# A hybrid decoder block on one core: weight halves and activation tiles moved by 64 bytes against each other

## The chip, the cores and the metric

The kernel runs on one NeuronCore of a Trainium2 chip, as one launch. The metric is the device time of an execution in microseconds; 1 us is 1000 ns. Every number on the kernel before comes from three timed executions, or from one further execution that the hardware profiler recorded.

## The reference, cut to what matters

For 256 tokens of width 2048 the block computes, in float32 (cut to its matrix products):

```python
h = rms_norm(x, attn_norm_g)
q, k, v, u, gate_attn, gate_ssm = split(h @ w_in + b_in)
attn = sliding_window_attention(q, k, v, sinks)
y_val, y_gate = split(gelu(s5_ssm(u, ...)) @ w_glu + b_glu)
ssm = y_val * sigmoid(y_gate)
merged = sigmoid(gate_attn) * (attn @ w_branch_attn) + sigmoid(gate_ssm) * (ssm @ w_branch_ssm)
x = x + merged @ w_out
val, gate = split(rms_norm(x, ffn_norm_g) @ w_up)
x = x + (val * gelu(causal_depthwise_conv(gate))) @ w_down
return rms_norm(x, final_norm_g)
```

Nearly all of the arithmetic is in seven products of 256 tokens with large weight matrices: `w_in`, `w_branch_attn`, `w_glu`, `w_branch_ssm`, `w_out`, `w_up`, `w_down`.

## The kernel before

**Units.** All weights are cut into 416 units of 128 partitions x 1024 columns, in the order that `_units` (line 58) lists: `q0`, `u`, `kv`, `q1`, `ga`, `gs` (parts of `w_in`), `A` (`w_branch_attn`), `glu`, `S` (`w_branch_ssm`), `o` (`w_out`), `up0` to `up21` (`w_up`), `dn0` to `dn3` (`w_down`). A unit is eight blocks of 128 x 128. The loop at line 1009 goes through the units; TensorE is fed by it without a break, and the other work (the state-space scan, attention, norms) is put in between by generators (`fill`, line 802) as soon as a hand-kept clock of each engine says that its inputs are there.

**Split numbers.** Each float32 weight is split into two parts that TensorE multiplies at its fast float32 rate: `load` (line 220) brings a unit into one of four buffers `raw`, each as soon as the buffer's last unit is split; `prep` (line 231) lets ScalarE round it into `whi` (the upper half) and VectorE compute `wlo = raw - whi` (the lower half). There are five buffers of each (`LOOK = 5`), used in turn. The activations are split in the same way into an upper and a lower tile. A product is hi x hi + hi x lo + lo x hi.

**Two shapes of the inner loop.** TensorE holds a block of weights (128 x 128) and streams columns of activations past it; while one block is in use, the next block is loaded (profile engine PEld). Where the accumulator has 256 columns (all stages up to `up0`, and `dn3`), three matmuls of 256 columns are made per block, lines 1064 to 1066: `whi` past the upper activations, `whi` past the lower, `wlo` past the upper. Where it has 512 columns (`up1` to `up21`, `dn0` to `dn2`; `double`, line 1051), the activation tile holds upper and lower side by side, and two matmuls are made:

```python
PE.matmul(acc[:, c], hi[:, kk, c], both, ...)              # 512 columns, upper half of the weights
PE.matmul(acc[:, c, 0:T], lo[:, kk, c], mh[:, k], ...)     # 256 columns, lower half
```

So in the wide stages a load of a lower half lies under each matmul of 512 columns, and a load of an upper half under each of 256. In the narrow stages a load lies under every matmul of 256 columns. This text calls a matmul, from its start to the start of the next, a step, and the two steps of a block in the wide stages a pair.

**Where the tiles lie.** Each tile has an address, the byte at which it starts in every partition. Tiles are laid down one behind the other by pools, so a tile that grows moves all behind it. Blocks of weights lie 512 bytes apart within a unit, and the parts of activation tiles 1024 or 2048 bytes apart, so a tile's start over the last multiple of 128 bytes (its offset, below) is that of each of its operands too. In the kernel before `whi` and `wlo` have offset 0 in all five buffers; `xg` and `x2g` (lines 183 and 968: inputs of `q` to `gs`, and of `up`) have 64; `ath`/`atl` (input of `A`), `su` (`glu`), `mh`/`ml` (`o`) and `H` (`dn`) have 0; `sy` (`S`) has 96.

Of the kernel before, what the change touches and what calls it, by code (L numbers as in the profile page):

```python
# [8 lines left out]
F32 = mybir.dt.float32  # L9
F32R = mybir.dt.float32r  # L10
# [5 lines left out]
P = 128  # L16
T = 256
NK = 16
D_MODEL = 2048
D_FF = 5632  # L20
NFF = D_FF // P
EPS = 1e-6
NJ = 16
LOOK = 5
# [33 lines left out]
def _units():  # L58
# [7 lines left out]
    out = pair(block("q0", NK, 4), block("u", NK, 4)) + block("kv", NK, 2) + block("q1", NK, 4)  # L66
    for n, K in (("ga", NK), ("gs", NK), ("A", 8)):
        for c in range(3 if n == "A" else 4):
            out += block(f"{n}{c}", K, 4)
# [68 lines left out]
def hybrid_block_kernel(  # L138
# [17 lines left out]
    base = ctx.enter_context(tc.tile_pool(name="base", bufs=1))  # L156
    strm = ctx.enter_context(tc.tile_pool(name="strm", bufs=1))
# [22 lines left out]
    ident = base.tile([P, P], F32, tag="ident", name="ident")  # L180
    rs = base.tile([P, T], F32, tag="rs", name="rs1")
    hb = base.tile([P, 40], F32, tag="hb", name="hb")
    A = base.tile([P, NK, 2, T], F32R, tag="A", name="xg")
    Ah, Al = A[:, :, 0], A[:, :, 1]
    mid_cm, mid = open_pool("mid")
    X = mid.tile([P, NK, T], F32, tag="tS", name="x_in")
# [18 lines left out]
    units = _units()  # L205
# [25 lines left out]
    def prep(i, parts=1):  # L231
        if i >= NU:
            return
        raw = raws.pop(i)
        clk_a.ns = max(clk_a.ns, clk_pe.ns if i >= LOOK else 0.0, arrive.pop(i))
        hi = strm.tile([P, 1024], F32R, tag="whi", name=f"whi{i}", bufs=LOOK)
        lo = strm.tile([P, 1024], F32R, tag="wlo", name=f"wlo{i}", bufs=LOOK)
        n = 1024 // parts
        for j in range(parts):
            sl = slice(j * n, (j + 1) * n)  # L240
            S.copy(hi[:, sl], raw[:, sl])
            clk_v.ns = max(clk_v.ns, clk_a.ns + 130.0)
            V.tensor_tensor(lo[:, sl], raw[:, sl], hi[:, sl].bitcast(F32), op=ALU.subtract)
        prepped[i] = (hi, lo, clk_v.ns)
        if i >= 4:
            load(i + 4)
# [30 lines left out]
        V.tensor_tensor(sq[:, 0:2], sq[:, 0:2], sq[:, 2:4], op=ALU.add)  # L277
        V.tensor_tensor(sq[:, 0], sq[:, 0], sq[:, 1], op=ALU.add)

# [1 line left out]
    V.memset(ones, 1.0)  # L281
    V.memset(eps, EPS)
    S.activation(hb[:, 0:1], eps, AF.Sqrt)
# [10 lines left out]
    warm = bank("at", P)  # L294
    for i in range(WARM):
        PE.matmul(warm, ones, ones, start=True, stop=True)
# [1 line left out]
    st = {}  # L298
    bq8 = base.tile([P, 8], F32, tag="bq8", name="bq8")

    def ev_proj(name, acc, dst, scale, biases, func, fscale):
# [6 lines left out]
        def rest():  # L308
            for i in range(m):
                yield "A", None  # L310
                S.activation(dst[:, i], dst[:, i], func, bias=biases[i], scale=fscale)
# [17 lines left out]
        ks = range(4 * b, 4 * b + 4)  # L329
        ev_proj(f"{n}{b}", acc, dst[:, 4 * b : 4 * b + 4], None, [hb[:, off + i : off + i + 1] for i in ks], AF.Tanh, 0.5)  # L330

# [1 line left out]
    def g_norm1():  # L333
        sq = mid.tile([P, 2, 4, T], F32, tag="tA", name="sq1")
        v = p1.tile([P, 2], F32, tag="sv1", name="sv1")
# [2 lines left out]
        dg = p1.tile([P, 2, P], F32, tag="ul", name="dg")  # L338
        yield "A", None
        S.activation(sq[:, 0], X[:, 0:4], AF.Square)  # L340
        for b in range(1, 4):
            yield "A", None
            S.activation(sq[:, 1], X[:, 4 * b : 4 * b + 4], AF.Square)
# [23 lines left out]
        S.copy(rs, ps[1].rearrange("p h t -> p (h t)"))  # L367
        st["rs"] = True

# [1 line left out]
    def g_ssm():  # L371
        sp = p1.tile([P, 22, NJ], F32, tag="sp", name="sp")
        ki = p1.tile([P, NJ], I32, tag="ki", name="ki")
# [59 lines left out]
        dt, mag, th, n, r, sn, cn, sh, abr, abi, zr, zi, t1, t2, t3, t4, den, ar = [t(i) for i in range(18)]  # L433
# [19 lines left out]
        tt(zr, t1, den, ALU.mult)  # L453
        yield "D", None

        E = base.tile([P, 2, NJ, P], F32, tag="X", name="E")
        V.memset(E[:, 0, :, 0:1], 1.0)
        V.memset(E[:, 1, :, 0:1], 0.0)
        V.tensor_copy(E[:, 0, :, 1:2], cn.unsqueeze(2))
        V.tensor_copy(E[:, 1, :, 1:2], sn.unsqueeze(2))  # L460
        L = 1
        while L < P:
# [3 lines left out]
            for j0 in range(0, NJ, jn):  # L466
                js = slice(j0, j0 + jn)
                a = p1.tile([P, 2, jn, cnt], F32, tag="T1", name=f"ea{L}_{j0}", bufs=2)
                b = p1.tile([P, 2, jn, cnt], F32, tag="T2", name=f"eb{L}_{j0}", bufs=2)
                lr = E[:, 0:1, js, L : L + 1].to_broadcast([P, 2, jn, cnt])  # L470
                li = E[:, 1:2, js, L : L + 1].to_broadcast([P, 2, jn, cnt])
                src = E[:, :, js, 1 : cnt + 1]
# [153 lines left out]
        y_ev(3)  # L626
        st["y3"] = True

# [1 line left out]
    def g_attn():  # L630
        yield "D", wait_for("kv", "q0")
        qT = st["qT"]
# [88 lines left out]
    def g_norm2():  # L721
        sq, ps = st["sq"], {}
        yield "D", None
        fold(sq)

        def total():
            ps[0] = bank("at", 2)
            for h in range(2):
                PE.matmul(ps[0][:, h : h + 1], sq[:, 0, h * P : (h + 1) * P], ones[:, 0:1], start=True, stop=True)

        def spread():
            ps[1] = bank("at", 2, P)
            for h in range(2):
                PE.matmul(ps[1][:, h], ones, dg[:, h], start=True, stop=True)

        yield "D", later(total)
        n2 = mid.tile([P, 3, 2], F32, tag="ath", name="n2")
        dg = mid.tile([P, 2, P], F32, tag="atl", name="dg2")
        rstd(ps[0], n2[:, 0], n2[:, 1], n2[:, 2])
        for h in range(2):  # L740
            V.tensor_scalar(dg[:, h], ident, n2[:, 2, h : h + 1], None, op0=ALU.mult)
        yield "A", later(spread)
        st["rs2"] = base.tile([P, T], F32, tag="rs", name="rs2")
        S.copy(st["rs2"], ps[1].rearrange("p h t -> p (h t)"))
        close_pool(st["p2cm"])
        close_pool(mid_cm)
        st["ffncm"], fp = open_pool("ffn")
        st["ffn"] = fp
        st["H"] = fp.tile([P, NFF, 2, T], F32R, tag="H", name="H")
        st["gb"] = fp.tile([P, 2, T + 2], F32, tag="gb", name="gb")  # L750
        V.memset(st["gb"][:, :, 0:2], 0.0)

# [172 lines left out]
    def evac(name, acc):  # L925
        if name == "u":
            ev_u(acc)
        elif name == "kv":
            ev_kv(acc)
            spawn(g_attn(), dve=5000.0, act=5000.0, first=True)  # L930
        elif name[0] == "q":
            ev_q(int(name[1]), acc)
        elif name[:2] == "ga":
            if st["tA"] is None:
                st["tA"] = mid.tile([P, NK, T], F32, tag="tA", name="tA")
            ev_gate("ga", st["tA"], int(name[2]), 0, acc)
        elif name[:2] == "gs":
            if st["tS"] is None:
                st["tS"] = mid.tile([P, NK, T], F32, tag="tS", name="tS")
            ev_gate("gs", st["tS"], int(name[2]), 16, acc)  # L940
        elif name[0] == "A":
            ev_A(4 * int(name[1]) + (2 if name[-1] == "y" else 0), 2 if len(name) == 3 else 4, acc)
        elif name[0] == "S":
            ev_S(int(name[1]), acc)
        elif name[:3] == "glu":
            if name == "glu0":
                assert not gens and not aux
                close_pool(p1_cm)
                st["p2cm"], st["p2"] = open_pool("p2")
                p2 = st["p2"]  # L950
                st["mh"] = p2.tile([P, NK, T], F32R, tag="mh", name="mh")
                st["ml"] = p2.tile([P, NK, T], F32R, tag="ml", name="ml")
                st["sy"] = base.tile([P, 2, 4, T], F32R, tag="X", name="sy")
            ev_glu(int(name[3]), acc)
        elif name[0] == "o":
            ev_o(int(name[1]), acc)
        elif name[:2] == "up":
            ev_up(int(name[2:]), acc)
        elif name[:2] == "dn":
            ev_dn(int(name[2]), acc)  # L960

    def begin(name):
        if name == "glu0":
            finish("su1")
        elif name == "o0":
            st["X"] = base.tile([P, NK, T], F32, tag="X", name="xres")
            nc.gpsimd.dma_start(st["X"], xT)
            A2 = base.tile([P, NK, 2, T], F32R, tag="A", name="x2g")
            st["A"], st["Ah"], st["Al"] = A2, A2[:, :, 0], A2[:, :, 1]
            A2 = mid.tile([P, 2, 4, T], F32, tag="tA", name="sqA")  # L970
            st["sq"], st["sq2"] = A2[:, 0], A2[:, 1]
        elif name == "dn0":
            A3 = base.tile([P, 2, NK, T], F32, tag="A", name="xo_sq")
            st["xo"] = A3[:, 0]
            st["sq"], st["sq2"] = A3[:, 1, 0:4], A3[:, 1, 4:8]

# [32 lines left out]
    for i, (name, K, m, k0, kw) in enumerate(units):  # L1009
        if k0 == 0:  # L1010
# [11 lines left out]
            if name[:2] == "dn" or name[:2] == "up" and name != "up0":  # L1022
                if name == "up1":
                    close_pool(ax_cm)
                    wide_cm, pool = open_pool("wide_b", space=PSUM, side="right")
                    wide = [pool]
                elif name == "up2":
                    close_pool(acc_cm)
                    wide_cm2, pool = open_pool("wide_a", space=PSUM, side="left")
# [3 lines left out]
            elif name == "kv":  # L1033
                accs[name] = bank("pq", m, T)
            elif name[:2] == "A3":
                accs[name] = bank("at" if name == "A3x" else "pq", m, T)
# [6 lines left out]
        hi, lo, ready = prepped.pop(i)  # L1043
        clk_pe.ns = max(clk_pe.ns, ready)
        hi = hi.rearrange("p (k m c) -> p k m c", k=kw, m=m)
        lo = lo.rearrange("p (k m c) -> p k m c", k=kw, m=m)
# [11 lines left out]
        for kk in range(0 if double else kw):  # L1058
            k = k0 + kk
            for c in range(m):  # L1060
                o = acc[:, c, 0:T]
                first = k == 0 and (c % 2 == 0 or name == "dn3")
                last = k == K - 1
# [27 lines left out]
        if k0 + kw == K and name == "dn2":  # L1091
            spawn(g_pre(), 2)

# [1 line left out]
    Hh, Hl = st["H"][:, :, 0], st["H"][:, :, 1]  # L1095
    Xr, xo, sq = st["X"], st["xo"], st["sq"]
    n3 = st["ffn"].tile([P, 3, 2], F32, tag="cy", name="n3")
# [12 lines left out]
    for n in range(4):  # L1110
        o = (aux, acc)[n % 2][:, n // 2 * 2, 0:T]
# [23 lines left out]
    for c0, c1 in zip(cuts, cuts[1:]):  # L1135
        o = xo[:, c0:c1]
# [102 lines left out]
```

## Time and profile before

| what | value |
|---|---|
| three timed executions | 1251.51, 1252.0, 1253.03 us (median 1252.0) |
| profiled execution, first to last instruction | 1249.7 us |
| stage `o`, 768 steps of 256 columns | 92.15 us |
| stages `up`, from 502.60 us on | 482.71 us, 2757 matmuls |
| stages `dn`, up to the tail | 241.27 us, 1512 matmuls |
| VectorE, ScalarE busy | 856.9 us, 620.0 us |

The profiled execution's own time is its span of 1249.7 us; the timed executions hold some 2.3 us more around it. PE is TensorE's matmuls, PEld its weight loads, DVE VectorE, ACT ScalarE. The recorded duration of a matmul reaches past the start of the next one, since matmuls are pipelined; what a step costs is read from the chain of work that ended last (start, length, number of matmuls).

### The profile page before, as it was taken

What the parts mean: (1) busy time and instruction counts of PE and PEld (TensorE: products, weight loads), DVE (VectorE), ACT (ScalarE), POOL (GpSimd) and SP (SyncE); (2) the same over time, 40 slices, a digit from 0 to 9 for tenths busy, and PEclk for the clock granted to TensorE, in tenths of its full rate; (3) what the DMA queues carried; (4) which work ended last, traced back from release to release, by engine and by line L of the source; (5) the groups of instructions that cost most, each with busy time, mean ns of one, the idle gap of its engine ahead of it and who ended that gap; (6) DMA issues with size and microseconds to landing.
All of it is one profiled execution on the core that took longest, in us unless ns stands there. A gap on an engine that the chain in (4) does not pass through costs nothing.

```text
span 1249.7 us, 20901 instructions
## 1 busy us (share of the span) xinstructions
PE 1235.7 (99%) x8476; PEld 1125.1 (90%) x8476; DVE 856.9 (69%) x1220; ACT 620.0 (50%) x865; POOL 10.4 (1%) x24
## 2 busy tenths in 40 slices
PE   9999999999999999999999999999999999999996
PEld 8999899989999999988888888888888888888996
DVE  7988998989878556567677666676666755454543
ACT  7676555554444445445445454454455534343531
POOL 0000000000000000000000000000000000000000
PEclk9999999999999999999999999999999999999998
DMA  8565444444446654654655646546456475646451
GB/s 315 205 203 185 162 152 162 140 164 169 153 169 227 207 180 163 205 183 152 214 174 179 216 145 216 189 159 222 159 187 214 140 235 165 208 165 208 165 184 68
DMA packets 64896, 228.29 MB, mean 183 GB/s; under 512 B 7648, under 2 KB 9056, under 8 KB 64672
## 3 DMA queue, kind: packets, MB, share of 16 engines
q1 hardware_dynamic: 63648, 223.55, 52.9%
q0 software_dynamic: 1152, 3.41, 0.9%
q8 instruction: 66, 1.08, 0.4%
q14 instruction: 30, 0.25, 0.1%
HBM read 224.31 MB, written 2.10 MB: 181 GB/s over the span
## 4 chain that ended last, share of the span: by engine, by line
PE 98%; DVE 1%; DMA 0%; ACT 0%; SPq 0%; issue 0%; DVEq 0%
PE acc_up L132 40%; PE acc_dn L132 20%; PE acc_o L132 7%; PE acc_gs L132 7%; PE acc_ga L132 7%; PE acc_q L132 3%; PE acc_A L132 3%; PE pq L132 2%; PE at L132 2%; PE acc_u L132 2%; PE acc_S L132 2%; PE yp L132 1%; PE acc_glu L132 1%; PE aux L132 1%; DMA raw<-in_wst_dram 0%; DVE xo_sq L132 0%
## 5 line engine op out<-in xcount | busy, mean ns | idle before, releaser
L132 DVE TENSOR_TENSOR wlo<-raw,whi 128x1024 fp32r<-128x1024 f32 (+2 forms) x421 | 501.4, 1209 | 277.0 <-ACT whi L132 274.0
L132 ACT CAST whi<-raw 128x1024 fp32r<-128x1024 f32 (+2 forms) x421 | 429.5, 1038 | 420.4 <-PE acc_dn L132 111.3
L132 PE MATMUL acc_up<-x2g,whi 128*128 128x512 f32 (+1 forms) x1472 | 497.2, 387 | 0.0
L132 PE MATMUL acc_up<-x2g,wlo 128*128 128x256 f32 x1408 | 395.4, 281 | 0.0
L132 PEld LDWEIGHTS acc_up<-x2g,whi 128*128 128x128 f32 x1472 | 272.1, 188 | 62.4
L132 PEld LDWEIGHTS acc_up<-x2g,wlo 128*128 128x128 f32 x1408 | 264.3, 188 | 0.0
L132 PE MATMUL acc_dn<-H,whi 128*128 128x512 f32 (+1 forms) x856 | 245.9, 355 | 0.0
L132 PE MATMUL acc_dn<-H,wlo 128*128 128x256 f32 x692 | 194.7, 281 | 0.0
L132 PEld LDWEIGHTS acc_dn<-H,whi 128*128 128x128 f32 x856 | 150.4, 189 | 24.8
L132 PEld LDWEIGHTS acc_dn<-H,wlo 128*128 128x128 f32 x692 | 131.3, 190 | 0.0
L132 PE MATMUL acc_gs<-xg,whi 128*128 128x256 f32 x512 | 91.4, 282 | 0.0
L132 PE MATMUL acc_ga<-xg,whi 128*128 128x256 f32 x512 | 91.2, 282 | 0.0
L132 PEld LDWEIGHTS acc_gs<-xg,whi 128*128 128x128 f32 x512 | 77.8, 189 | 2.6 <-issue 1.7
L132 PEld LDWEIGHTS acc_ga<-xg,whi 128*128 128x128 f32 x512 | 77.6, 188 | 2.8 <-issue 2.0
L132 PE MATMUL acc_o<-mh,whi 128*128 128x256 f32 x256 | 72.5, 283 | 0.0
L132 PE MATMUL acc_o<-ml,whi 128*128 128x256 f32 x256 | 72.5, 283 | 0.0
L132 PE MATMUL acc_o<-mh,wlo 128*128 128x256 f32 x256 | 72.5, 283 | 0.0
L132 PE MATMUL acc_gs<-xg,wlo 128*128 128x256 f32 x256 | 71.3, 278 | 0.0
L132 PE MATMUL acc_ga<-xg,wlo 128*128 128x256 f32 x256 | 71.2, 278 | 0.0
L132 PEld LDWEIGHTS acc_o<-ml,whi 128*128 128x128 f32 x256 | 49.2, 192 | 0.0
L132 PEld LDWEIGHTS acc_o<-mh,whi 128*128 128x128 f32 x256 | 49.2, 192 | 0.0
L132 PEld LDWEIGHTS acc_o<-mh,wlo 128*128 128x128 f32 x256 | 49.2, 192 | 0.0
(212 smaller groups left out, 1371.7 us busy)
## 6 DMA issues: line engine op xcount, KB each, us to landing
raw<-in_wst_dram SPq DMA_DIRECT2D x415, 512.0 KB, 4.2
xres<-in_xT_dram POOLq DMA_DIRECT2D x1, 2048.0 KB, 9.9
x_in<-in_xT_dram SPq DMA_DIRECT2D x7, 256.0 KB, 5.9
out_dram<-xo_sq SPq DMA_DIRECT2D x7, 256.0 KB, 2.4
br<-in_ssmb_dram POOLq DMA_DIRECT2D x3, 256.0 KB, 4.2
raw<-in_wst_dram SPq DMA_DIRECT2D x2, 256.0 KB, 3.4
cT<-in_ssmc_dram SPq DMA_DIRECT2D x1, 512.0 KB, 6.3
us<-ul POOLq DMA_DIRECT2D x16, 32.0 KB, 3.1
```

Of the source, the lines that this page charges most:

```text
L132: return fn(*a, **k)
```

## The change

The change alters addresses alone. On each of the five engines the instructions and their order are the same before and after; no matmul, load, copy or transfer is added, removed or moved in order.

- A helper `shifted` makes a tile 16 elements (64 bytes) larger and uses it from element `off` on. It is used for `xg`, `E`, `xres`, `xo_sq` (off 0), `x2g` and `H` (off 16) and `sy` (off 8).
- A `wlo` buffer becomes 1040 elements long, so that the five begin at offsets 0, 64, 0, 64, 0, and `prep` uses 1024 of them from element 0 or 16 on: in the stages `up` and `dn` so that the lower half lies at offset 64, in all others at 0.
- Since tiles grow, those behind them move. `ath`, `atl`, `su`, `mh`, `ml` come to lie at offset 64, and the small tiles of the state-space branch and of attention all move by 64, moving and stationary operands alike. `raw`, which began at a multiple of 256 bytes, begins 128 bytes over one.

Offsets in bytes over a multiple of 128, before and after:

| stage | activations | `whi` | `wlo` |
|---|---|---|---|
| `q`, `u`, `kv`, `ga`, `gs` | 64, 64 | 0, 0 | 0, 0 |
| `A`, `glu`, `o` | 0, 64 | 0, 0 | 0, 0 |
| `S` | 96, 64 | 0, 0 | 0, 0 |
| `up` | 64, 0 | 0, 0 | 0, 64 |
| `dn` | 0, 0 | 0, 0 | 0, 64 |

The core of the diff:

```diff
-    A = base.tile([P, NK, 2, T], F32R, tag="A", name="xg")
+
+    def shifted(pool, tag, name, dims, dtype, off=0, room=16):
+        n = math.prod(dims)
+        t = pool.tile([P, n + room], dtype, tag=tag, name=name)[:, off : off + n]
+        names = "abcd"[: len(dims)]
+        return t.rearrange(f"p ({' '.join(names)}) -> p {' '.join(names)}", **dict(zip(names, dims)))
+
+    A = shifted(base, "A", "xg", (NK, 2, T), F32R)
...
-        lo = strm.tile([P, 1024], F32R, tag="wlo", name=f"wlo{i}", bufs=LOOK)
+        o = 16 if (i % LOOK % 2 == 0) == (units[i][0][:2] in ("up", "dn")) else 0
+        lo = strm.tile([P, 1040], F32R, tag="wlo", name=f"wlo{i}", bufs=LOOK)[:, o : o + 1024]
...
-        E = base.tile([P, 2, NJ, P], F32, tag="X", name="E")
+        E = shifted(base, "X", "E", (2, NJ, P), F32)
...
-        st["H"] = fp.tile([P, NFF, 2, T], F32R, tag="H", name="H")
+        st["H"] = shifted(fp, "H", "H", (NFF, 2, T), F32R, 16)
...
-                st["sy"] = base.tile([P, 2, 4, T], F32R, tag="X", name="sy")
+                st["sy"] = shifted(base, "X", "sy", (2, 4, T), F32R, 8)
...
-            st["X"] = base.tile([P, NK, T], F32, tag="X", name="xres")
+            st["X"] = shifted(base, "X", "xres", (NK, T), F32)
...
-            A2 = base.tile([P, NK, 2, T], F32R, tag="A", name="x2g")
+            A2 = shifted(base, "A", "x2g", (NK, 2, T), F32R, 16)
...
-            A3 = base.tile([P, 2, NK, T], F32, tag="A", name="xo_sq")
+            A3 = shifted(base, "A", "xo_sq", (2, NK, T), F32)
```

## The prediction

> **What bounds the kernel now.** I read the page first: who is busy, the clock, and the chain of work that ended last. DVE is VectorE and ACT ScalarE.
>
> ```profile
> PE 1235.7 (99%) x8476; PEld 1125.1 (90%) x8476; DVE 856.9 (69%) x1220; ACT 620.0 (50%) x865; POOL 10.4 (1%) x24
> PEclk9999999999999999999999999999999999999998
> PE 98%; DVE 1%; DMA 0%; ACT 0%; SPq 0%; issue 0%; DVEq 0%
> ```
>
> TensorE's matmuls make up 98% of the chain, at the full granted clock. Nobody feeds it late, so the time is the number of steps by the length of a step, and the change leaves the number as it is. The question is whether a step's length depends on where its operands lie. The chain in order of time answers that for 256 columns (start, length, number of matmuls):
>
> ```profile
> 12.96 2.72 PE acc_q L132 x24
> 52.15 10.88 PE pq L132 x96
> 101.55 13.82 PE acc_ga L132 x120
> 167.34 5.30 PE acc_ga L132 x45
> 363.15 8.64 PE acc_glu L132 x72
> 371.79 8.41 PE acc_S L132 x71
> 395.41 92.15 PE acc_o L132 x768
> ```
>
> The matmul has one shape throughout, and yet the step differs. Activations at offset 64, weights at 0: 2.72/24 = 113.3 ns in `q`, 10.88/96 = 113.3 in `kv` (pq), 115.2 and 117.8 in the two pieces of `ga`. Activations and weights both at 0: 8.64/72 = 120.0 in `glu`, 92.15/768 = 120.0 in `o`. In between, at 96 (`S`): 118.5. So 113.3 is the free step, equal offsets cost 6.7 ns, and unequal ones cost nothing in one mode and 4.5 ns in another (117.8). As 256 columns take 113.3 ns, 6.7 ns is the time of 15 of them, and 16 columns are 64 bytes: it looks as if one stream waits until the other has passed its piece of 64 bytes.
>
> Now the wide stages, 58% of the span, with the recorded duration of one matmul by shape:
>
> ```profile
> 502.60 482.71 PE acc_up L132 x2757
> 985.31 241.27 PE acc_dn L132 x1512
> L132 PE MATMUL acc_up<-x2g,whi 128*128 128x512 f32 x1344 | 474.9, 397 | 0.0
> L132 PE MATMUL acc_up<-x2g,wlo 128*128 128x256 f32 x1408 | 395.4, 281 | 0.0
> L132 PE MATMUL acc_dn<-H,whi 128*128 128x512 f32 x528 | 186.6, 399 | 0.0
> L132 PE MATMUL acc_dn<-H,wlo 128*128 128x256 f32 x692 | 194.7, 281 | 0.0
> ```
>
> Of the 2757 matmuls of `up`, 2688 are 1344 pairs, and 69 belong to `up0` (7.8 us at 113.3): (482.71 - 7.8)/1344 = 353.3 ns a pair. Of `dn`, 456 belong to `dn3` (54.7 us at 120.0): (241.27 - 54.7)/528 = 353.3. Unequal offsets in `up`, equal ones in `dn`, and the same pair. Free, 768 columns would take three times 113.3, 340.0. So each pair loses 13.3 ns, twice the 6.7 of above, whichever the offsets, as long as both weight halves have the same one.
>
> **Why, by the loads.** The first matmul of 512 columns, alone in its window, with its neighbours; the free 256-column group of `kv`; and the loads of `up`, whose last column is the idle time before them:
>
> ```profile
> L132 PE MATMUL acc_up<-x2g,whi 128*128 128x512 f32 x1 | 0.4, 388 | 0.0
> L132 PE MATMUL pq<-xg,whi 128*128 128x256 f32 x64 | 10.9, 276 | 0.0
> L132 PEld LDWEIGHTS acc_up<-x2g,whi 128*128 128x128 f32 x1472 | 272.1, 188 | 62.4
> L132 PEld LDWEIGHTS acc_up<-x2g,wlo 128*128 128x128 f32 x1408 | 264.3, 188 | 0.0
> ```
>
> A load takes 188 ns, longer than a narrow step: there each load follows on the one before, 75 ns into its step (188 - 113). I call that chained. The load of a lower half, under 512 columns, is chained too (idle 0.0). The load of an upper half, under 256 columns, is not: before it the loader stood idle, 62.4 us/1344 = 46 ns each time, so it begins with its step. I call that fresh. The first matmul of 512 columns came straight out of the narrow rhythm of `up0`, chained and with unequal offsets, and lasted 388, which is 276 and the 112 of another 256 columns: free. All later ones last 397, and their 256-column partners 281 where 276 is free: +9 and +5, together the 13.3 within rounding. So unequal offsets suit a chained load, and a fresh one collides with them; I conclude that a fresh load wants equal offsets, and that its delay puts the next chained one out of step.
>
> **The change part by part.** *Wide stages.* `x2g` and `H` at 0, `whi` at 0, `wlo` at 64: the fresh load of `whi` gets equal offsets and the chained load of `wlo` unequal ones. If both collisions go, the pair is 340.0: (1344 + 528) x 13.3 = 24.9 us saved. No row of before shows mixed halves. The ends are 340.0, the free pair, and above it 360, since the narrow steps at equal offsets lose 6.7 for each of 256 columns (3 x 120.0). I take 340.0: the first 512-column row shows that half of it exists. Against it: in `dn` the fresh loads have equal offsets already and their matmuls still average 281. There the chained loads collide (399 against 388), which may disturb the fresh ones.
>
> *Narrow stages that go from equal to unequal.* `A` 384 steps, `glu` 96, `o` 768, so 1248. They come to the offsets of `q` and `ga`, between 113.3 and 117.8; I take 115.2, the longest `ga` piece quoted: 1248 x 4.8 = 6.0 us (2.7 to 8.3). `S`, 192 steps from 118.5: 0.6 us (0.1 to 1.0).
>
> *Narrow steps with mixed halves.* `up0` (192 steps) and `dn3` (528 with its tail) have chained loads alone; of three, two bring `whi` (equal, 120.0) and one `wlo` (unequal, 113.3): 117.8 on average. `dn3`: 528 x 2.2 = 1.2 us saved; `up0`, from 115.2: 192 x 2.6 = 0.5 us lost.
>
> *All else* stays: `q` to `gs` keep their offsets, and the small matmuls of attention and the scan have both operands moved by 64. At a pair of 340 a unit takes 2.72 us where it took 2.83. The other engines in the wide stages (busy us of PE, PEld, DVE, ACT, POOL, then clock, DMA share, GB/s):
>
> ```profile
> 430.00:700.00 270.00, 270.00 (x1754) 245.04 (x1753) 175.15 (x207) 132.64 (x163) 0.00 (x0) 1.00 0.55 185
> raw<-in_wst_dram SPq DMA_DIRECT2D x415, 512.0 KB, 4.2
> xres<-in_xT_dram POOLq DMA_DIRECT2D x1, 2048.0 KB, 9.9
> 3.07 5.71 DMA raw<-in_wst_dram
> ```
>
> VectorE is busy 65% and the DMA engines 55%; 4% more is no bound. The `raw` buffers now begin 128 bytes over a multiple of 256. `xres` already begins off such a multiple (224 over), and its 2048 KB land in 9.9 us, not slower per byte than `raw` (512 KB in 4.2), so I cost that at nothing. Only the first load, 5.71 us on the path, has no cover. The Trainium skill, "DMA: Bandwidth & Descriptors", section "How a descriptor splits into AXI transactions", speaks against the change here: a descriptor that doesn't start on 256 bytes needs one transaction more, 17 in place of 16 for 4096 bytes. By that page the uncovered load would be an estimated 0.4 us longer and the sum as much less; the `xres` row doesn't show it.
>
> **Sum.** 24.9 + 6.0 + 0.6 + 1.2 - 0.5 = 32.2 us. The profiled span of 1249.7 would become 1217.5. The timed median is 1252.0, 2.3 more, which stays: 1219.8, rounded to 1220. With the narrow bounds (3.4 to 10.0) this case spans 1217 to 1224.
>
> **Rivals.**
> 1. *Half of it.* One of the two collisions goes, the pair is 346.7: 12.5 + 7.3 = 19.8, 1232. For it: the two are separate in the rows (+9, +5). Against: the later one seems caused by the earlier.
> 2. *The pair doesn't move.* For it: 353.3 at two quite different offsets; the +9 on 512 columns could come with the shape once it runs, and the first one be an exception. Then the narrow stages alone gain: 1252.0 - 7.3 = 1244.7 (1242 to 1249).
> 3. *Slower: the load of `whi` collides at equal offsets whether fresh or chained*, as every narrow step of `o` does, and sets the next load off its place. The pair becomes the 360 of three steps of `o`: 1872 x 6.7 = 12.5 lost, 7.3 won, 1257. It decides from a pair of 353.3 + 7300/1872 = 357.2 on. For it: `up` gives up the unequal offsets that are the better ones in every narrow row. Against: `dn`, all equal, is at 353.3 and not at 360.
> 4. *Slower: the period is 256 bytes, not 128.* In before `xg` lies 192 over a multiple of 256 and the weights 0; after, `whi` lies at 128, and `q` to `gs`, 2208 steps, would fall to 120.0: 2208 x 4.8 = 10.6 lost, the gains in `A`, `glu` and `o` not made, and if the pairs stay too, 1263. Against: 6.7 ns fits 64 bytes, not 128.
> 5. *The change does nothing*, since loads and moving columns don't meet in memory: 1252. The rows speak against it: 113.3 and 120.0 for one shape. The Trainium skill, "TensorE: Matmul & The Clock Gate", Part 2, says so of the load of the next block: it "doesn't steal SBUF read bandwidth from the running matmul". By that rule the sum is 0; the trace disagrees with it, if it is the load that the columns meet.
>
> **How the numbers follow.** Forecast 46%, rival 1 14%, rival 2 20%, rival 3 11%, rival 4 4%, rival 5 5%. Forecast and rivals 1 and 2 hold 80%, so the range runs from 1215 (the forecast's lower end less the 1.5 us by which the runs differ) to 1249. A measurement of this kernel can tell about 0.2%, 2.5 us, from no change. Faster: 0.46 + 0.14 + 0.20 = 0.80. Same: 0.05. Slower: 0.11 + 0.04 = 0.15.
>
> **What would show it.** Right: the 512-column group of `up` at a mean of 388 and its partners at 276, `up` and `dn` alike; the idle time before the loads of `whi` down to some 39 ns each (227 - 188); the chain piece of `o` at 87 to 90 us. Rival 1: one of the two groups alone shorter. Rival 2: 397 and 281 stay. Rival 3: 403 and 283 or more. Rival 4: `kv` above 113.3. The forecast is wrong if the pair is above 347.

## The result, and the profile after

| | before | after |
|---|---|---|
| timed executions | 1251.51 to 1253.03 us (four) | 1244.58, 1244.64, 1245.79 us |
| median | 1252.1 us | 1244.6 us |
| profiled execution, first to last instruction | 1249.7 us | 1244.0 us |
| last matmul's start, from the span's start | 1240.4 us | 1234.9 us |

The ratio is 0.9946, with an interval of 0.993 to 0.9962: 0.5% faster, where the prediction said 2.6%. A fourth execution of after took 1333.55 us at a granted clock of 0.85 and is left out here; the profiled one shows a clock of 0.95, but its steps have the length that experiment 2 has at 1.00 (117.8 ns in `o`).

The page of after: busy time of the engines, the shares of the chain that ended last, the shapes in the wide stages, and the transfers of `raw`.

```profile
PE 1230.2 (99%) x8476; PEld 1127.4 (91%) x8476; DVE 857.7 (69%) x1220; ACT 620.0 (50%) x865; POOL 10.4 (1%) x24
PE 96%; DVE 2%; DMA 1%; ACT 1%; issue 0%; SPq 0%; DVEq 0%; ACTq 0%
L132 PE MATMUL acc_up<-x2g,whi 128*128 128x512 f32 x1344 | 468.2, 392 | 0.0
L132 PE MATMUL acc_up<-x2g,wlo 128*128 128x256 f32 x1408 | 395.5, 281 | 0.2 <-DVE wlo L132 0.2
L132 PEld LDWEIGHTS acc_up<-x2g,whi 128*128 128x128 f32 x1472 | 271.9, 188 | 56.5
raw<-in_wst_dram SPq DMA_DIRECT2D x415, 512.0 KB, 4.3
```

The same 8476 matmuls; TensorE is still the bound, and the time is still their number by the length of a step. The loader stands idle for 56.5 us ahead of the loads of upper halves where it was 62.4, and the matmul of 512 columns went from 397 to 392 ns, but its partner of 256 columns still averages 281. One of the two groups alone is shorter: that is the sign which the prediction gave for its rival 1. The chain in order of time (start, length, number of matmuls):

```profile
13.21 2.80 PE acc_q L132 x24
53.72 11.31 PE pq L132 x96
104.18 14.34 PE acc_ga L132 x120
400.98 90.46 PE acc_o L132 x768
506.82 219.78 PE acc_up L132 x1284
983.60 237.90 PE acc_dn L132 x1512
```

Three things are to be seen. `kv` (pq) and the long piece of `ga`, whose offsets over 128 did not change, went from 113.3 and 115.2 ns a step to 11.31/96 = 117.8 and 14.34/120 = 119.5 (117.8 over the whole of `ga`). `o` came down from 120.0 to 90.46/768 = 117.8, not to 115.2. And the pair of the wide stages is shorter, by less than foretold: in `dn`, with 456 steps of `dn3` at 118.5, (237.90 - 54.0)/528 = 348.2 ns.

Summed over every step of a stage, from one matmul's start to the next one's (us; in brackets the mean step or pair in ns, waits left out):

| stage | before | after | difference | forecast |
|---|---|---|---|---|
| `up1` to `up21`, `dn0` to `dn2`: 1872 pairs | 661.4 (353.3) | 652.5 (348.3) | -8.9 | -24.9 |
| `q`, `u`, `kv`, `ga`, `gs` | 263.3 (115.0) | 269.1 (117.7) | +5.8 | 0 |
| `A`, `glu`, `o` | 150.6 (119.9) | 148.1 (117.9) | -2.6 | -6.0 |
| `S` | 23.6 (118.4) | 23.3 (116.3) | -0.3 | -0.6 |
| `dn3` with its tail | 63.6 (120.0) | 62.8 (118.5) | -0.8 | -1.2 |
| `up0` | 22.2 (114.4) | 22.8 (117.8) | +0.6 | +0.5 |
| everything else | | | +0.6 | 0 |
| sum | | | -5.6 | -32.2 |

So two things have to be explained: why the pair is 348.3 and not 340, and why the stages that were to stay as they were lost 5.8 us.

**In two units of five the change does the opposite of what it says.** Here are the starts of three units of `up1`, each of 8 pairs (start, recorded length, line, operation, tiles); the matmuls between them are left out:

```profile
517.57 0.39 PE L132 MATMUL acc_up<-x2g,whi 128*128 128x512 f32 x1
...
523.17 0.39 PE L132 MATMUL acc_up<-x2g,whi 128*128 128x512 f32 x1
...
531.50 0.39 PE L132 MATMUL acc_up<-x2g,whi 128*128 128x512 f32 x1
```

From the first to the second lie two units, 16 pairs of 350.0 ns; from the second to the third three units, 24 pairs of 347.1. Over all of `up`, by the unit's number modulo 5, the pairs are 346.7, 349.4, 351.0, 347.2 and 347.1 ns. The addresses in the built kernel tell why: the pool hands out the five `wlo` buffers in the order first, fifth, fourth, second, third, while the formula in `prep` takes them to come first to fifth. For units 1 and 2 modulo 5 the lower half therefore lies at 0 in the wide stages and at 64 in the narrow ones. The table of offsets ahead of the prediction holds for the other three units only.

### The profile page after: what moved, and what is told of

It is laid out like the page before. It is cut to its first block, busy times and chain, and to the rows that moved or that the text cites. A ratio compares the mean times of both kernels' runs of the same rounds, so it can differ in the third digit from the quotient of the medians.

```text
span 1244.0 us, 20901 instructions
## 1 busy us (share of the span) xinstructions
PE 1230.2 (99%) x8476; PEld 1127.4 (91%) x8476; DVE 857.7 (69%) x1220; ACT 620.0 (50%) x865; POOL 10.4 (1%) x24
## 4 chain that ended last, share of the span: by engine, by line
PE 96%; DVE 2%; DMA 1%; ACT 1%; issue 0%; SPq 0%; DVEq 0%; ACTq 0%
PE acc_up L132 37%; PE acc_dn L132 19%; PE acc_ga L132 7%; PE acc_gs L132 7%; PE acc_o L132 7%; PE acc_q L132 3%; PE acc_A L132 3%; PE pq L132 2%; PE at L132 2%; PE acc_u L132 2%; PE acc_S L132 2%; PE yp L132 1%; DMA raw<-in_wst_dram 1%; PE acc_glu L132 1%; DVE wlo L132 1%; PE aux L132 1%
## 5 line engine op out<-in xcount | busy, mean ns | idle before, releaser
L132 PE MATMUL acc_up<-x2g,whi 128*128 128x512 f32 (+1 forms) x1472 | 491.1, 383 | 0.0
L132 PEld LDWEIGHTS acc_up<-x2g,whi 128*128 128x128 f32 x1472 | 271.9, 188 | 56.5
L132 PE MATMUL acc_dn<-H,whi 128*128 128x512 f32 (+1 forms) x856 | 242.5, 350 | 0.0
L132 PEld LDWEIGHTS acc_dn<-H,whi 128*128 128x128 f32 x856 | 149.4, 188 | 22.2
L132 ACT ACTIVATE cy<-cy 128x512 f32<-128x512 f32 x22 | 13.9, 632 | 69.9 <-DVE cy L132 69.9
L132 PEld LDWEIGHTS acc_gs<-xg,wlo 128*128 128x128 f32 x256 | 48.1, 188 | 0.0
```

Of the source, the lines that this page charges most:

```text
L132: return fn(*a, **k)
```

## The experiments

From here on *distance* is the start of the activations less the start of `whi`, and *lower distance* the start of `wlo` less that of `whi`, both modulo 256 bytes. Before: `q` to `gs` and `up` have distance 192, `A`, `glu`, `o` and `dn` 0, `S` 224, lower distance 0 everywhere. After: 64 in `q` to `gs`, `A`, `glu`, `o`, 192 in `S`, and 128 in `up` and `dn`; the lower distance in the wide stages is 64 or 192 in three units of five, and 0 in two. Theories: (A) the prediction's, offsets modulo 128; (B) the period is 256 bytes; and, of the pair, whether the wrong units alone keep it from 340.

**1. The formula mended.**

```diff
-        o = 16 if (i % LOOK % 2 == 0) == (units[i][0][:2] in ("up", "dn")) else 0
+        o = 16 if (i % LOOK in (0, 1, 4)) == (units[i][0][:2] in ("up", "dn")) else 0
```

> The changed kernel, with one number list edited so that every lower half lies where the change says: at offset 64 in up and dn, at 0 elsewhere. In the changed kernel itself the five buffers are handed out in the order 1st, 5th, 4th, 2nd, 3rd, so the units whose number is 1 or 2 over a multiple of 5 have it the other way round. Theory A, that slip is what spoiled the forecast: pairs 347 ns or less in every unit (they average 348.3 now), narrow steps of q to gs back from 117.8 to 113 to 115, so 1232 to 1236 us, or 1222 if pairs reach 340. Theory B, the lower half's place modulo 128 is not what counts (256 or 512 is): narrow steps stay near 118 and pairs at 347 to 350, so 1242 to 1246 us.

Measured: 1241.7 us (1240.23 to 1243.03), ratio to before 0.9913, interval 0.9899 to 0.9926. From its chain:

```profile
104.60 14.39 PE acc_ga L132 x120
367.31 8.16 PE acc_glu L132 x72
504.86 166.08 PE acc_up L132 x980
```

Of the 980 matmuls 69 are narrow ones of `up0` (8.15 us), so the pair is (166.08 - 8.15)/455.5 = 346.7 ns, and so it is in every unit but for waits. The slip costs 1.6 ns a pair, 1872 x 1.6 = 3.0 us, and the medians differ by 2.9. The two agree partly by chance: in the traced execution 2.6 us of waits for lower halves in `up` and `dn` (0.4 in after) take most of those 3.0 us back, and `A`, `glu` and `o` give 1.1 us. The slip isn't what keeps the pair from 340, and `ga` stays at 119.9 in this piece and 117.9 over the stage. Theory A falls. `glu`, at the distance of 64 that gave 118.3 in after, runs at 8.16/72 = 113.3 here, and `A` goes between 118 and 113 ns within the stage: one distance, two step lengths. Experiments 4 and 6 come back to this.

**2. The activation tiles alone.** The kernel before with a gap of 64 bytes ahead of the pool that holds `ath` to `mh` and, later, `H`:

```diff
+    gap = ctx.enter_context(tc.tile_pool(name="gap", bufs=1))
+    gap.tile([P, 16], F32, tag="gap", name="gap")
```

> The kernel before with one unused tile of 64 bytes ahead of the pools of attention and FFN: ath, atl, su, mh, ml and H come to lie at offset 64, all weights stay at 0, at equal places modulo 4096. Nothing of the wide stages' mixed halves is in it. Theory A (offset modulo 128 decides): steps of o, A and glu go from 120.0 to between 113.3 and 117.8 as in ga, dn3 likewise, pairs of dn stay at 353.3; 1243 to 1248 us. Theory B (the place modulo 256 or 512 decides; the tiles come 64 above the weights' place where xg lies 64 below): o anywhere from 113 to 120, pairs of dn may move by some ns.

Measured: 1246.25 us (1245.68 to 1248.28), ratio 0.9954, interval 0.9941 to 0.9968. Its chain:

```profile
101.39 13.82 PE acc_ga L132 x120
392.58 90.45 PE acc_o L132 x768
498.41 482.71 PE acc_up L132 x2757
981.12 240.26 PE acc_dn L132 x1512
```

`ga`, not touched, is as in before in this piece (over the stage 114.0 against 115.2); `o`, at distance 64, is 117.8. `up` is the same to the hundredth, and in `dn` only `dn3` moves (120.0 to 117.8; the pair stays 353.3). So moving these tiles gives all of the narrow gain, and the loss in `q` to `gs` comes from the change's other part, the start of `whi` at 128 over 256 with `xg` where it was.

**3. The steps by themselves.** A kernel in which one pair of weight blocks, upper and lower, and one row of activations are multiplied in both rhythms, at distances in steps of 64 bytes over 512; nothing waits for anything within a segment.

```python
for a in range(8):
    for b in range(8):
        m, h, l = 16 * a, hi[:, 0:128], lo[:, 16 * b : 16 * b + 128]
        segment("n" + "abcdefgh"[a] + "abcdefgh"[b], [(h, m, 256), (h, m + 256, 256), (l, m, 256)] * 24)
...
        segment("w" + "abcdefgh"[a] + "abcdefgh"[b], [(h, m, 512), (l, m, 256)] * 32)
```

> Not the block: a kernel of TensorE steps alone, nothing of the reference is computed. For each of 64 places (activations and lower half each at 0, 64, ... 448 bytes over a multiple of 512, upper half at 0) it makes 72 narrow steps (upper, upper, lower) and 32 wide pairs (512 columns by the upper, 256 by the lower). Theory A (period of 128 bytes): the tables repeat every 128 bytes in both directions; unequal offsets give 113.3 to 117.8 narrow, equal ones 120.0; wide pairs 353.3 where both halves have one offset, 340 to 347 with activations equal to the upper half and unequal to the lower. Theory B: they don't repeat at 128 but at 256 or 512. Theory C (not the memory but the work of the other engines beside it): all places give one number.

The chain has one row for each segment: the second letter is the distance (a 0, b 64, up to h 448), the third the lower distance. Narrow segments, of 72 steps, lower distance 0:

```profile
19.92 8.91 PE naa L105 x72
92.42 8.76 PE nba L105 x72
164.43 8.81 PE nca L105 x72
236.69 8.46 PE nda L105 x72
307.52 8.91 PE nea L105 x72
523.94 8.46 PE nha L105 x72
```

Less 0.27 to 0.30 us for the end of the last matmul, the step is 120.0, 117.8, 118.7 and 113.3 ns at distances 0, 64, 128 and 192, and 120.0 and 113.3 again 256 bytes on (the other two likewise, in rows not shown). With a period of 128 the first and third row would be equal, and the second and fourth: they aren't. Theory B holds for the activations, and this row of four gives what the narrow stages of after measured: 192 (113.3) to 64 (117.8) in `q` to `gs`, 0 (120.0) to 64 in `A`, `glu` and `o`. The other engines stand all but still here and the numbers are the same, so their work is not what makes a step long. The lower distance counts too: at 192 the step is 113.3 with 0 or 128 and about 118 with 64 or 192. Wide segments, 32 pairs each:

```profile
594.78 11.38 PE waa L105 x64
699.73 11.18 PE wbb L105 x64
781.14 11.52 PE wca L105 x64
792.90 11.38 PE wcb L105 x64
874.89 11.59 PE wda L105 x64
910.24 11.19 PE wdd L105 x64
```

Less 0.3, a pair is 346.7 at (0, 0), 340.0 at (64, 64), 350.8 at (128, 0), 346.7 at (128, 64), 353.3 at (192, 0) and 340.0 at (192, 192) (the last in one of the four segments at that place modulo 256; the other three gave 350). The third and fourth are the wrong and the right units of after, which measured 349 to 351 and 347; the fifth is `up` of before. So 340 exists, but not where the change puts the tiles. One row does not fit: (0, 0) is `dn` of before, and there the pair is 353.3.

**4. The two best places of that table.** The kernel before, with distance 192 and lower distance 0 in the narrow stages up to `o`, and 64 and 64 in `up` and `dn`. The five lower halves lie in one tile, so that the lower distance is the same in each (the moves of the activation tiles are left out here):

```diff
+            lows.append(strm.tile([P, LOOK * 1024 + 16], F32R, tag="wlo", name="wlo"))
+        o = i % LOOK * 1024 + (16 if units[i][0][:2] in ("up", "dn") else 0)
+        lo = lows[0][:, o : o + 1024]
```

> The kernel before with its tiles put where the table of steps was fastest, counted from the upper half modulo 256: activations of every narrow stage at 192 with the lower half at 0, x2g and H at 64 with the lower half at 64. The lower halves are five places in one tile, so that all lie alike modulo 4096; in up and dn they are used from element 16 on. Theory B (the place modulo 256 counts, and the table holds in the block): pairs 340.0, narrow steps of A, glu, o and S 113.3, up0 and dn3 117.8: 24.9 + 8.3 + 1.0 + 1.2 - 0.6 = 34.8 less, 1217 us. Rival (pairs of that place lock into the other state that the table also showed, 350): 6.2 + 9.9, 1236 us. Rival (theory A, the offset modulo 128 alone): the same offsets modulo 128 in the wide stages as mixed halves turned round, 346.7: 1230 us.

Measured: 1244.57 us, from 1237.66 to 1250.77 in six executions; ratio 0.9927, interval 0.9901 to 0.9954. The starts of units of 8 pairs, in `up7` and in `up8`, and the matmuls by the lower half in `o`:

```profile
657.26 0.40 PE L132 MATMUL acc_up<-x2g,whi 128*128 128x512 f32 x1
...
660.06 0.40 PE L132 MATMUL acc_up<-x2g,whi 128*128 128x512 f32 x1
...
673.95 0.39 PE L132 MATMUL acc_up<-x2g,whi 128*128 128x512 f32 x1
...
676.67 0.39 PE L132 MATMUL acc_up<-x2g,whi 128*128 128x512 f32 x1
...
L132 PE MATMUL acc_o<-mh,wlo 128*128 128x256 f32 x256 | 73.8, 288 | 6.2 <-DVE wlo L132 6.2
```

2.80 us, 350 ns a pair, and 2.72 us, 340 ns a pair, with the same addresses. The trace has 350.0 from `up1` into `up7`, then 340.0 until `up10`, then 350.0 to the end of `dn2`, and each switch comes with a stall of TensorE (the last with one of 1.1 us); two stalls in between switched nothing. So one place of the tiles has more than one stable rhythm, and a disturbance can move the engine from one to another. `A`, `glu` and `o`, at the distance at which `q` to `gs` run at 114.5 or less, stayed at 117.7 to 117.8, likely for the same reason. There were also waits for lower halves: 6.2 us idle ahead of matmuls in `o`, in three stalls between 472 and 490 us. There the start in the single tile goes from element 0 to 16, and the built program shows what follows: the lower half of a unit of `up0` is written over the first 16 elements of that of a unit of `o` which TensorE has yet to use, in three units. The matmul waits for that write and then multiplies by the wrong 16 elements, so this version is good for its times only. The steps behind the stalls take 213 ns, at a mean granted clock of 0.84 between 472 and 494 us, and `o` loses 9.9 us against experiment 5. The expected gain was lost to the rhythms and to these stalls; the traced execution is the slowest of the six.

**5. The narrow part of that, without the single tile.** The kernel before with a gap of 192 bytes ahead of the same pool, and `sy` at distance 192.

```diff
+    gap.tile([P, 48], F32, tag="gap", name="gap")
...
-                st["sy"] = base.tile([P, 2, 4, T], F32R, tag="X", name="sy")
+                st["sy"] = base.tile([P, 8 * T + 56], F32R, tag="X", name="sy")[:, 56:].rearrange("p (s k t) -> p s k t", s=2, k=4)
```

> The kernel before with the tiles of attention and FFN moved by 192 bytes and sy to 192, weights untouched: every narrow stage at 192 over the weights modulo 256, wide stages at 192, lower halves at 0. Theory B: o, A, glu and S at 113.3 to 115 (not the 117.8 that they had at 64), pairs of dn 353.3: 8 to 10 us less, 1242 to 1244. Theory A: 192 and 64 are one offset modulo 128, so 117.8 again as in the run with a move by 64, 1246 us.

Measured: 1242.29 us (1241.59 to 1246.55), ratio 0.9927, interval 0.9913 to 0.9941. Its chain:

```profile
102.06 13.82 PE acc_ga L132 x120
393.45 90.45 PE acc_o L132 x768
```

`o` takes 117.8 ns a step, though `ga`, at the same distance, has 115.2 in this piece. The pair stays at 353.3. The time is what theory B expected and the steps are not: the execution that was traced took 1246.55 us, the longest of the four, and with `o` at 117.8 it is where experiment 2 is. The other three took 1241.59 to 1242.79; that they had the shorter steps is likely, but none of them was traced.

**6. Rhythms, counted.** The kernel of steps alone again, at distances of 16 bytes, and with one place started in twelve ways: six narrow triples or wide pairs at another distance go ahead of 32 triples or pairs at the place in question.

```python
for k in range(12):
    segment("v" + L[k], narrow(4 * k, 0, 6) + wide(16, 16, 32))   # place (64, 64)
...
for k in range(12):
    segment("s" + L[k], wide(4 * k, 0, 6) + narrow(48, 0, 32))    # distance 192
```

> Steps alone, nothing of the reference computed. Narrow steps at 16 places of the activations, 16 bytes apart over 256, each twice, once with a wide step in their middle; wide pairs at places around activations 64, lower half 64, by 16 bytes; then the pair (64, 64), the pair (0, 0) and the narrow place 192 twelve times each, started behind different steps. Theory B: the narrow table has one low stretch around 192 and its values go by pieces of 64 bytes; the pair (64, 64) is 340.0 whatever came before. Rival (several stable rhythms at one place): the pair (64, 64) falls to 340 behind some starts and to 350 behind others, (0, 0) to 346.7 or 353.3, and the narrow place 192 to 113.3 or 117.8.

Two starts of each of the two places:

```profile
753.67 13.27 PE vb L105 x82
780.68 13.60 PE vd L105 x82
1083.32 13.27 PE sb L105 x108
1096.83 13.68 PE sc L105 x108
```

By the starts of the matmuls, (64, 64) settled at 340.0 from nine starts and at 350.0 from three; (0, 0) at 353.3 from five and 346.7 from seven, which clears up the row that did not fit; distance 192 in the narrow rhythm at 113.3 from seven and 117.8 from five. Of the 16 narrow places only 112 and 192 gave 113.3 (8.48 us for 72 steps; the others 8.73 to 8.92), so theory B's low stretch around 192, and values that go by pieces of 64 bytes, did not come out.

**7 and 8. Every distance of 16 bytes in the wide rhythm**, each from two starts (`x` out of the block before, `y` after six narrow steps), and, in the second kernel, three narrow places from twelve starts each.

```python
for a in range(0, 8):      # the second kernel: 8 to 16
    for b in range(16):
        segment("w" + L[a] + L[b] + "x", wide(4 * a, 4 * b, 16))
        segment("w" + L[a] + L[b] + "y", narrow(28, 0, 2) + wide(4 * a, 4 * b, 16))
```

> Steps alone, nothing of the reference computed: 16 wide pairs at each place of activations 0 to 112 and lower half 0 to 240 bytes over the upper half modulo 256, by 16 bytes, each from a standing start and once more behind six narrow steps at 112. Several stable rhythms: the two starts give one value at some places and two at others; few places give 340.0 from both. One rhythm for each place: the two starts always agree.

> Steps alone, nothing of the reference computed: as the run before for activations 128 to 240. Then narrow steps, twelve times each behind different wide steps, at activations 112 with the lower half at 0, at 112 with 128, and at 192 with 128. Several stable rhythms: 192 gives 113.3 and 117.8 in turn, as it did before; 112 gives 113.3 each time if that place has one rhythm alone.

The pair runs from 340 to 363 ns over the table. It is 340 or 341 from both starts at three places only: (112, 48), (112, 208) and (16, 80). Rows of the first (`d` is 48) and of (64, 64):

```profile
897.33 5.88 PE weex L105 x32
903.45 6.44 PE weey L105 x38
1505.08 5.73 PE whdx L105 x32
1511.04 6.45 PE whdy L105 x38
```

Less 0.29 for the end, 5.73 us is 16 pairs of 340, and 5.88 is 16 of 350: the first place gives 340 from both starts, (64, 64) here only from the second. In the narrow rhythm of the second kernel, distance 112 with lower distance 0 settled at 113.3 from all twelve starts, 112 with 128 at 118.2 from all twelve, and 192 with 128 at 113.3 from all twelve.

**9 and 10. Distance 112 everywhere**, with lower distance 48 in the wide stages, and then with lower distance 0 throughout. Here the upper halves start 16 bytes over a multiple of 64, where the kernels of steps alone had them at a multiple of 64. Of the first one's diff, the part on the weights:

```diff
+            halves.append(strm.tile([P, LOOK * 1024 + 16], F32R, tag="whi", name="whi"))
+            halves.append(strm.tile([P, LOOK * 1024 + 56], F32R, tag="wlo", name="wlo"))
+        o = i % LOOK * 1024
+        hi = halves[0][:, o + 4 : o + 1028]
...
+        o += 0 if name[:2] in ("up", "dn") and name not in ("up0", "dn3") else 52
+        lo = halves[1][:, o : o + 1024]
```

> The kernel before with every activation tile 112 bytes over the upper half modulo 256, the place that gave 113.3 a narrow step behind each of twelve starts, and the lower half at 0 in narrow stages and at 48 bytes in wide ones, where the table of pairs has 340.0 from both starts. If the table carries over: pairs 340.0 (24.9 us), A, glu and o 113.3 (8.3), S 1.0, dn3 528 x 6.7 = 3.5, q to gs 113.3 without the 117.8 rhythm (2208 x 2 = 4.4): 42 less, 1210 us. Rival (the rhythm is set in the block by what other work does to TensorE, not by the place): pairs at 346.7 to 350 in parts as in the mapped run, 1222 to 1240 us. Rival (a faster TensorE runs into the weights' transfers): matmuls wait for lower halves, above 1215 with the shorter steps in the trace.

> The same with the lower half at 0 everywhere: no mixed halves. The table has 353.3 for the pair at activations 112, lower half 0, so only the narrow gains are left, 17 less: 1235 us. If instead mixed halves are not what makes the pair short, it is as fast as the run beside it.

Measured: 1260.14 us (1259.12 to 1262.25), ratio 1.0068, interval 1.0055 to 1.008; and 1254.64 us (1254.1 to 1257.01), ratio 1.0025, interval 1.0014 to 1.0035. Both are slower than before. Two rows of the first one's chain, and its wait for lower halves:

```profile
53.20 11.52 PE pq L132 x96
403.90 92.16 PE acc_o L132 x768
L132 PE MATMUL acc_dn<-H,wlo 128*128 128x256 f32 x692 | 195.0, 282 | 6.1 <-DVE wlo L132 6.1
```

`kv` and `o` take 120.0 ns a step where the steps alone took 113.3 at the same distance from every start; the pairs take 346.7, and 349.3 in the second (waits left out). The table was not carried over. What is different is the start of the weights modulo 64, and that many blocks and activations take turns. The steps of `q` to `gs` alone lose some 9 us against before in both. The first one's pairs gain 12.5 us and lose 11.9 again, most of it in three stalls and the slow steps behind them at the end of `dn2` (1162 to 1181 us): there the lower halves go from element 0 to 52 of their places, and three of them are written over as in experiment 4. The second, with the same single tile and one start throughout, has no such stall.

**11. The whole kernel moved by 32 bytes**, every distance kept, to see whether the place itself counts:

```diff
     base = ctx.enter_context(tc.tile_pool(name="base", bufs=1))
+    base.tile([P, 8], F32, tag="gap", name="gap")
```

> The kernel before with a gap of 32 bytes ahead of all its tiles: every address 32 bytes higher, every distance between operands as before. If only the distance of two operands decides, nothing moves: kv at 113.3 ns a step, o at 120.0, the pair at 353.3, 1252 us within 2.5. If the absolute place has a part too, as the run with the upper halves at 16 over a multiple of 64 let it seem, the steps change, by up to 6.7 ns a step and 13.3 a pair either way: anything from 1225 to 1270 us.

Measured: 1252.07 us (1251.15 to 1253.28), ratio 1.0003, interval 0.9994 to 1.0012. Its chain:

```profile
52.29 10.88 PE pq L132 x96
395.55 92.15 PE acc_o L132 x768
502.74 482.71 PE acc_up L132 x2757
985.44 241.27 PE acc_dn L132 x1512
```

Every one of these lengths is that of before, to the hundredth. A shift of 32 bytes changes nothing, so distances decide. What a shift of 16 does was not tried by itself, and why the narrow steps of 9 and 10 take 120.0 stays open.

**12. Both parts at places that the steps alone found good.** The kernel of experiment 1, with distance 192 in `q` to `gs`, `A`, `glu` and `o`, lower distance 0 or 128 there, and the wide stages left at distance 128 with lower distance 64 or 192. The steps alone gave one value from every start at 192 with 128 (113.3) and at both wide places (346.7), and two values at 192 with 0. The five lower buffers stay apart:

```diff
-    A = shifted(base, "A", "xg", (NK, 2, T), F32R)
+    A = shifted(base, "A", "xg", (NK, 2, T), F32R, 16)
...
+    mid.tile([P, 32], F32, tag="gap", name="gap")
...
-        E = shifted(base, "X", "E", (2, NJ, P), F32)
+        E = shifted(base, "X", "E", (2, NJ, P), F32, 0, 0)
...
-                st["sy"] = shifted(base, "X", "sy", (2, 4, T), F32R, 8)
+                st["sy"] = shifted(base, "X", "sy", (2, 4, T), F32R)
...
-            st["X"] = shifted(base, "X", "xres", (NK, T), F32)
+            st["X"] = shifted(base, "X", "xres", (NK, T), F32, 0, 0)
...
-            A2 = shifted(base, "A", "x2g", (NK, 2, T), F32R, 16)
+            A2 = shifted(base, "A", "x2g", (NK, 2, T), F32R)
```

> The kernel after with its five lower buffers treated in the order in which they are handed out (as in the run that did what the change says), and with the activations of the narrow stages (but S) moved on, so that they lie 192 bytes over the upper halves by a multiple of 256, as in q to gs of before, and those of the wide stages 128, as after; all starts stay multiples of 32, and the upper halves lie at 64. If the distance modulo 256 decides, the 2208 steps of q to gs come back from about 117.5 ns to 113.3 to 115.5 (5 to 9 us less than 1241.7), the pairs stay at 346.7, and A, glu and o, 1248 steps, go to 113.3 to 117.8 (0 to 6 us less): 1228 to 1237 us. If the absolute place decides, the steps need not repeat: 1242 or more.

Measured: 1230.41 us (1229.49 to 1231.31), ratio to before 0.983, interval 0.9817 to 0.9844: the fastest version here, and faster than after by 14 us. Its chain:

```profile
53.12 10.88 PE pq L132 x96
391.45 87.38 PE acc_o L132 x768
969.94 237.16 PE acc_dn L132 x1512
```

`kv` is back at 113.3, `o` is at 113.8 (114.3 for `ga` and 113.9 for `gs` over the stage), and the pair is (237.16 - 54.0)/528 = 346.9. Here `A`, `glu` and `o` are in the fast rhythm, with lower distances of 0 and 128 in turn, where experiment 5 with 0 alone had them in the slow one. Against before, `q` to `gs` save 1.6 us, `A`, `glu` and `o` 7.5, the pairs 10.9, and all steps together 20.0.

## Why the prediction was right and wrong

**Right: the frame.** TensorE bounds the kernel, the change moves addresses alone, and the step's length depends on them; matmuls fill 99% of the span after as before, and VectorE and the DMA engines did not become a bound. (The row quoted for them, 430 to 700 us, begins in `o`; within `up`, from 510 to 980 us, VectorE is busy 68% before and after.) The sign was right, and the time is within the range. The time of rival 2 came out, 1244.7, by coincidence and not by its mechanism: the pair did move, and `q` to `gs` gave 5.8 us back.

**Wrong: "offsets over the last multiple of 128 bytes".** This step stands under the whole working, and only 192, 0 and 224 over 256 were in the rows. Experiment 3 gives 118.7 at 128 against 120.0 at 0, and 113.3 at 192 against 117.8 at 64: the period is 256. Rival 4 named it, at 4%, and was dismissed because 6.7 ns fits 64 bytes; that says nothing on a period. It was right on the period and wrong on the size, since it took the new place to cost what equal offsets cost, 120.0, and 64 cost 117.7 here: 5.8 us lost in place of its 10.6. For the same reason `A`, `glu` and `o` reached 117.8, the least gain that the text allowed, and not the 115.2 taken: 2.6 us in place of 6.0.

**Wrong: "the pair is 340.0".** The term of 24.9 us measured 8.9. In the three units of five that are as the change describes them the pair is 347, and experiment 1 makes it 346.7 in all: that is the number of rival 1, half of the two collisions. In the others it is 349 to 351. The theory behind the step, a fresh load that wants equal offsets and a chained one that wants unequal ones, was made from a single matmul of 388 ns and does not survive: the table of experiment 3 has 340.0 at (64, 64) and at (192, 192), where the upper half is off by 64 and the lower half equal, the reverse of what the theory asks, and 346.7 at (128, 64), for which it says 340. The first matmul of 512 columns was likely free because it came out of another rhythm, and not by what its own offsets bring for good: experiment 6 shows that the same place settles in different rhythms after different starts.

**Not looked at: whether the code does what the table says.** That the change doesn't do what it says was counted as nothing among the rivals. The order in which a pool hands out its buffers could have been read from the built kernel; the cost was some 3 us by the medians of after and experiment 1 (1244.64 and 1241.70).

**No price seen: transfers that begin 128 bytes over a multiple of 256.** The median landing of `raw` is 4.3 us after and 4.2 before, the first load on the path lasts 5.86 us where it was 5.71, and the first matmuls of `q` come 0.25 us later (13.21 against 12.96). The Trainium skill, "DMA: Bandwidth & Descriptors", section "How a descriptor splits into AXI transactions", would have the uncovered first load an estimated 0.4 us longer; these runs can't tell that from nothing, since the load that stands first on the chain lasts 4.83 us in experiment 2 and 6.59 in experiment 5, in both of which `raw` was not moved. The Trainium skill, "TensorE: Matmul & The Clock Gate", Part 2, was weighed as the rule by which nothing would change, since the next load "doesn't steal SBUF read bandwidth from the running matmul". Experiment 3 speaks against it if it is the load that the columns meet: one shape, the same blocks, and 113.3 to 120.0 ns by the address alone. That it is the load is the likely reading, since the lower distance changes the step too (350.8 and 346.7 at distance 128), but no run took the loads away.

**Settled and open.** Shown: the period of 256 in the activations, the loss in `q` to `gs` by the move of `whi`, the two wrong units, more than one rhythm at one place, distances and not places at a shift of 32 bytes. Open: the mechanism behind the table, what sets the rhythm in the whole kernel (`glu` at distance 64 had 118.3 in after and 113.3 in experiment 1), and why distance 112 with weights 16 bytes off did so badly.

## What to carry to other kernels

Where TensorE is the bound and loads a new block for every matmul, measure the step at several distances between the tiles before moving any, over a whole period and from several starts: here a narrow step cost 113.3 to 120.0 ns and a pair 340 to 363 by address alone. Prefer a place that gives the same step from every start to one that is fastest from some, check it in the whole kernel (distance 112 gave 113.3 from every start alone and 120.0 there), and work out the addresses from the built kernel, not from the code's formula. A regularity read from three addresses is not a period: before extrapolating it, ask which other periods the same rows allow.

## What the runs showed of the hardware

The step's length repeats with 256 bytes in the distance of activations and weights (lower distance 0: 120.0 ns at 0 and 256, 113.3 at 192 and 448). One set of addresses has two or more steady rhythms (340.0 and 350.0, 346.7 and 353.3, 113.3 and 117.8 ns), each kept for hundreds of steps (350.0 in every unit from `up11` to `dn2` in experiment 4), and there the two switches came with a stall. The executions of that kernel lay 13 us apart (1237.66 to 1250.77) where those of most others agree within some 3; that the rhythms are the cause is likely, but only one execution of it was traced.
